# Moving the matmul operands by 64 bytes against each other in on-chip memory

## The chip, the cores and the metric

One core of a Trainium2 chip runs the whole program. The time is that of one execution on the device in microseconds (us), the median over runs. Five engines work side by side on a core: TensorE (in the profile PE, its weight loads PEld), VectorE (DVE), ScalarE (ACT), GpSimd (POOL) and SyncE (SP, which here only issues transfers).

## What is computed

Two network blocks in a row on a sequence of 256 tokens of width 2048, all in 32-bit floating point. Cut to the matrix products that fill the time:

```python
# first block
h = einsum('bsd,de->bse', x, w_in)            # 2048 -> 18688, in 16 pieces
merged = sum(sigmoid(g[i]) * (y[i] @ w_branch[i]) for i in range(4))   # 1024 -> 2048 each
x = layer_norm(ALPHA * x + merged @ w_out)
# second block
proj = rmsnorm(x) @ w_in_2                    # SSD and attention with forget gates
x = x + concat(y_ssd, y_fox) @ w_out_2
t = rmsnorm(x); q = t @ peer_wq               # picks 16 of 128 x 128 experts per head
x = x + (G * gelu(t @ u.T)) @ v               # all 16384 experts, G is zero where not picked
return rmsnorm(x)
```

## The kernel before

Every weight matrix is cut into chunks of 128 x 2048 numbers (1 MB). One list, `stream`, holds the 526 chunks in the order of the program, and one loop at the end of `_kern` (lines 1704 to 1720) goes through their halves. SyncE loads a chunk into `wr` (three buffers). For each half, ScalarE copies it into `wh`, rounded to the matmul's own 32-bit format, and VectorE puts the rest, `wr - wh`, into `wl` (`split`, line 292; four buffers each). The other operand is split into a high and a low part in the same way: `XH` and `XL` hold 16 x 256 numbers per partition (the normalized input, transposed), `YH` and `YL` 8 x 256 (the outputs of a branch). A product is then the sum of three matmuls: high by high, low by high, high by low.

There are four ways in which the halves are used. The text calls them T, Y, N and V:

- T (`T_chunk`, line 318): 128 columns of the weight half are loaded into the array and 256 columns of XH or XL stream past them. The trace names the streaming operand first: `XH,wh`, `XL,wh`, `XH,wl`.
- Y (`wb_chunk`, line 767): the same with YH and YL for `w_branch`, from the middle of the first block to its end.
- N (`N_chunk`, line 353): 128 columns of XH or XL are loaded and 512 columns of the weight half stream: `wh,XH` and so on. `w_out`, `w_out2` and some parts of the input projections are of this kind.
- V (`V_chunk`, line 1626): 128 columns of `whh` or `whl` (the weighted activations, split) are loaded and 512 columns of the weight half stream. It fills the last quarter of the program.

```python
for kk in range(8):                                                       # T_chunk
    k = half * 8 + kk
    PE.matmul(o, h[:, kk], XH[:, k], start=k == 0, stop=False)
    PE.matmul(o, h[:, kk], XL[:, k], start=False, stop=False)
    PE.matmul(o, l[:, kk], XH[:, k], start=False, stop=k == KT - 1)
```

TensorE takes its matmuls in program order. Between them stand smaller matmuls of the background work (attention, pooling, the choice of experts), which `bg()` puts in once in each half. Among these are `gb,ga` (in `g_gen`, line 1494), four at a time, 256 columns in the same format as the T matmuls, between two T matmuls of `uT`.

Tiles get their places in on-chip memory from pools, in the order in which the pools ask for them. The pool `per` (XH, XL, X, constants) comes first, then `wraw` with `wr`, `wspl` with `wh` and `wl`, and then the pools of the stages one over the other: `a1` with YH and YL, `a2`, `a3`, `w5`. Every tile that a matmul reads here is a multiple of 512 bytes long per partition, and the slices that one matmul takes begin at multiples of 512 bytes in it, so all matmuls of a kind see the same places modulo 512. In `a1` a tile `gap` of 704 bytes stands ahead of YH; the attention uses its first 64 bytes.

Of the kernel before, what the change touches and what calls it, by code (L numbers as in the profile page):

```python
# [6 lines left out]
F32 = mybir.dt.float32  # L7
# [9 lines left out]
P = 128  # L17
# [202 lines left out]
def kern(tc, A, out):  # L220
    nc = tc.nc
    with ExitStack() as ctx:
        ctx.enter_context(tc.manual_schedule())
        _kern(tc, nc, ctx, A, out)


def _kern(tc, nc, ctx, A, out):
    tasks = Tasks(4)
    V, SC, G, PE = Meter(nc.vector, tasks, "dve"), Meter(nc.scalar, tasks, "act"), nc.gpsimd, Meter(nc.tensor, tasks, "pe")
    per = ctx.enter_context(tc.tile_pool(name="per", bufs=1))  # L230
# [5 lines left out]

    XH = per.tile([P, KT, S], FR, name="XH")
    XL = per.tile([P, KT, S], FR, name="XL")
    X = [per.tile([P, D], F32, name=f"X{t}") for t in range(2)]
    cst = per.tile([P, 7, P], F32, name="cst")  # L240
    par = per.tile([P, N_PAR], F32, name="par")
# [13 lines left out]
    def pv(name, i=0, n=1):  # L255
        o, _ = PAR[name]
        return par[:, o + i:o + i + n]

    def row_ap(name):
        o, w = ROW[name]  # L260
        src = A["rows"]
        return bass.AP(tensor=src.tensor, offset=src.offset + o, ap=[[0, P], [1, w]])
# [55 lines left out]
    def T_chunk(evac):  # L318
        def fn(half, hi, lo):
# [5 lines left out]
            for kk in range(8):  # L325
# [4 lines that stand above are left out]
# [6 lines left out]
    def dtf_chunk(evac):  # L336
        def fn(half, hl, _):
# [4 lines left out]
            for kk in range(8):  # L342
                k = half * 8 + kk
                PE.matmul(o, w[:, kk], XH[:, k], start=k == 0, stop=False)
                PE.matmul(o, w[:, kk], XL[:, k], start=False, stop=k == KT - 1)
                if kk == 2:
# [6 lines left out]
    def N_chunk(kq, evac, korder=(0, 1, 2, 3), hold=False, lead=None):  # L353
        def fn(half, hi, lo):
# [6 lines left out]
            def part(t, kq, half, h, l):  # L361
                ts = slice(t * P, (t + 1) * P)
                for kk in range(2):
# [3 lines left out]
                    PE.matmul(ps[t], XH[:, k, ts], h[:, kk], start=first, stop=False)  # L367
                    PE.matmul(ps[t], XL[:, k, ts], h[:, kk], start=False, stop=False)
                    PE.matmul(ps[t], XH[:, k, ts], l[:, kk], start=False, stop=last)
# [45 lines left out]
    a1 = p1.enter_context(tc.tile_pool(name="a1", bufs=1))  # L415
    w1 = p1.enter_context(tc.tile_pool(name="w1", bufs=2))

    B4 = [a1.tile([P, 1024], F32, name=f"B4{i}") for i in range(4)]
    gap = a1.tile([P, 176], F32, name="gap")
    YH = a1.tile([P, 8, S], FR, name="YH")  # L420
    YL = a1.tile([P, 8, S], FR, name="YL")
    R = a1.tile([P, 8 * 286 + 8 * 272], F32, name="R")
# [7 lines left out]
    Q = VQ.rearrange("p (j t) -> p j t", j=8)  # L430
    U_ = X[0].rearrange("p (j t) -> p j t", j=8)
    GA = X[1].rearrange("p (j t) -> p j t", j=8)
    kT = a1.tile([P, S], F32, name="kT")
# [15 lines left out]
    def start_split():  # L449
        for g in range(4):  # L450
            SC.copy(XH[:, g * 4:(g + 1) * 4], xq[g])
            V.tensor_sub(XL[:, g * 4:(g + 1) * 4], xq[g], XH[:, g * 4:(g + 1) * 4].bitcast(F32))
            if g < 2:
# [87 lines left out]
    def conv_gen(ln):  # L541
# [13 lines left out]
        for stat in range(2):  # L555
# [4 lines left out]
            m = w1.tile([P, S], F32, name="cm")  # L560
            V.tensor_reduce(m, (sq if stat else CV).rearrange("p j t -> p t j"), axis=AX.X, op=OP.add)
            yield WAIT
# [102 lines left out]
    def attn_gen(u):  # L665
        def make(ln):
# [24 lines left out]
            m2 = sm[:, 0, :nq].rearrange("p (v j) -> p v j", v=2)  # L691
            V.tensor_reduce(sm[:, 0, :nq], L3, axis=AX.X, op=OP.max)
            V.tensor_tensor(m2, m2, sks, op=OP.max)
# [104 lines left out]
    for br, (_, need, ysrc) in enumerate(order):  # L798
# [4 lines left out]
        for jj in range(8):  # L803
            def pre_y(need=need, ysrc=ysrc, br=br):
# [5 lines left out]
                if br == 2:  # L810
                    nc.gpsimd.dma_start(X[0], A["xN"][0])
                    nc.gpsimd.dma_start(X[1], A["xN"][1])
                    nc.gpsimd.dma_start(GC.rearrange("p j t -> p (j t)"), row_ap("ln_g"))
# [16 lines left out]
    def split_M(a, b):  # L830
        for g in range(a, b, 2):
            s = slice(g, g + 2)
            SC.copy(XH[:, s], M[:, s])
            V.tensor_sub(XL[:, s], M[:, s], XH[:, s].bitcast(F32))

# [28 lines left out]
    def to_T(t, lnw, hooks={}):  # L864
        for k0 in range(0, KT, 2):
# [6 lines left out]
            for k in (k0, k0 + 1):  # L872
                V.scalar_tensor_tensor(XL[:, k, t * P:(t + 1) * P], p[:, k - k0], pv(lnw, k),
                                       hs[:, k - k0].bitcast(F32), op0=OP.mult, op1=OP.subtract)
# [964 lines left out]
```

## Time and profile before

| | |
|---|---|
| median of 3 runs | 3102.1 us (3099.98 to 3108.45) |
| the profiled execution, own time | 3096.91 us |
| its span, first to last instruction | 3095.2 us |
| mean granted clock of TensorE in it | 0.996 of 2.4 GHz |
| busy: TensorE, VectorE, ScalarE, GpSimd | 98%, 71%, 51%, 7% |
| read from main memory over the span | 601.53 MB |

The page of the profile gives busy time by engine, the chain of work that ended last (followed back from the last instruction), and the costliest groups of instructions with their count and mean duration. Matmuls are pipelined: a matmul of 256 columns is listed with some 280 ns, but the next one starts long before it ends. How fast they follow each other is read from a table by stretch, which counts the instructions of an engine in a stretch of time, or from the timeline.

### The profile page before, as it was taken

The numbers are of one execution on the slowest core, as the hardware profiler recorded it, in microseconds if no ns is written. First come the engines' busy times: TensorE is split into PE (matmuls) and PEld (weight loads), VectorE is DVE, ScalarE is ACT, GpSimd is POOL, SyncE is SP. The second block draws the span as 40 slices with busy tenths as digits, with TensorE's granted clock in tenths as the row PEclk, the third lists the DMA queues.
The fourth block names the chain that finished last, engine by engine and source line by source line (L and its number), as shares of the span: only waits on it lengthen the run. The fifth ranks groups of instructions, "written<-read, shape, count | busy, mean of one in ns | idle before, by whom it ended". The sixth has DMA issues, their size and how long they took to land.

```text
span 3095.2 us, 53096 instructions
## 1 busy us (share of the span) xinstructions
PE 3045.9 (98%) x21964; PEld 2843.4 (92%) x21964; DVE 2200.6 (71%) x3195; ACT 1575.5 (51%) x2199; POOL 220.2 (7%) x187
## 2 busy tenths in 40 slices
PE   8999999999999989998999999999999999999998
PEld 8899999999999869897899999999999888888887
DVE  8899865555555567766489989788796666666665
ACT  4443565434444445556454457667675444444444
POOL 0000000000000020100000012223140000000000
PEclk9999999999999989999999999999999999999999
DMA  7555555555555535434545665666658766666654
GB/s 274 184 196 198 180 190 188 196 189 203 182 202 191 184 129 180 175 130 143 190 150 189 220 218 197 253 250 220 254 203 326 275 243 229 247 246 250 241 215 150
DMA packets 92226, 640.61 MB, mean 207 GB/s; under 512 B 10272, under 2 KB 10448, under 8 KB 17744
## 3 DMA queue, kind: packets, MB, share of 16 engines
q1 hardware_dynamic: 78192, 559.06, 50.0%
q0 software_dynamic: 13504, 77.63, 6.9%
q8 instruction: 172, 2.82, 0.4%
q14 instruction: 70, 0.57, 0.1%
q10 hardware_dynamic: 288, 0.52, 0.0%
HBM read 601.53 MB, written 35.65 MB: 206 GB/s over the span
## 4 chain that ended last, share of the span: by engine, by line
PE 96%; DVE 2%; ACT 1%; issue 1%; DMA 0%; POOL 0%; SPq 0%; DVEq 0%; ACTq 0%
PE pm L216 92%; PE bg L216 4%; ACT wh L216 1%; DVE wl L216 0%; DMA wr<-w_in 0%; DVE X L216 0%; DVE XL L216 0%; POOL keys L1523 0%; DVE stg L216 0%; ACT XH L216 0%; DVE gb L216 0%; DVE PX L216 0%; ACT PX L216 0%; ACT L216 0%; ACT keys L216 0%
## 5 line engine op out<-in xcount | busy, mean ns | idle before, releaser
L216 DVE TENSOR_TENSOR wl<-wr,wh 128x1024 fp32r<-128x1024 f32 x1048 | 1291.0, 1234 | 820.5 <-ACT wh L216 817.0
L216 ACT CAST wh<-wr 128x1024 fp32r<-128x1024 f32 x1054 | 1109.0, 1053 | 1380.7 <-PE pm L216 1328.4
L216 PE MATMUL pm<-XH,wh 128*128 128x256 f32 x4976 | 1392.1, 280 | 8.3 <-ACT wh L216 8.3
L216 PE MATMUL pm<-XL,wh 128*128 128x256 f32 x4976 | 1382.1, 278 | 0.0
L216 PE MATMUL pm<-XH,wl 128*128 128x256 f32 x4960 | 1378.7, 278 | 0.9 <-DVE wl L216 0.9
L216 PEld LDWEIGHTS pm<-XH,wh 128*128 128x128 f32 x4976 | 940.8, 189 | 14.5 <-ACT wh L216 8.3
L216 PEld LDWEIGHTS pm<-XL,wh 128*128 128x128 f32 x4976 | 936.8, 188 | 1.0 <-issue 0.7
L216 PEld LDWEIGHTS pm<-XH,wl 128*128 128x128 f32 x4960 | 931.8, 188 | 1.4 <-DVE wl L216 1.4
L216 PE MATMUL pm<-wh,whl 128*128 128x512 f32 x1024 | 398.3, 389 | 0.0
L216 PE MATMUL pm<-wh,whh 128*128 128x512 f32 x1024 | 398.3, 389 | 0.0
L216 PE MATMUL pm<-wl,whh 128*128 128x512 f32 x1024 | 398.3, 389 | 0.0
L216 PEld LDWEIGHTS pm<-wl,whh 128*128 128x128 f32 x1024 | 192.2, 188 | 39.9
L216 PEld LDWEIGHTS pm<-wh,whl 128*128 128x128 f32 x1024 | 192.2, 188 | 39.9
L216 PEld LDWEIGHTS pm<-wh,whh 128*128 128x128 f32 x1024 | 192.2, 188 | 39.8
L216 PE MATMUL pm<-wh,XH 128*128 128x512 f32 x448 | 178.0, 397 | 0.0
L216 PE MATMUL pm<-wh,XL 128*128 128x512 f32 x448 | 176.7, 394 | 0.0
L216 PE MATMUL pm<-wl,XH 128*128 128x512 f32 x448 | 176.4, 394 | 0.0
L1523 POOL TENSOR_TENSOR keys<-cst,t 128x512 f32<-128x512 f32 x64 | 132.2, 2065 | 208.0 <-ACT ga L216 207.7
L216 PE MATMUL pm<-YH,wh 128*128 128x256 f32 x512 | 144.1, 281 | 0.0
L216 PE MATMUL pm<-YL,wh 128*128 128x256 f32 x512 | 143.7, 281 | 0.0
L216 PE MATMUL pm<-YH,wl 128*128 128x256 f32 x512 | 143.7, 281 | 0.0
L216 DVE SCALAR_TENSOR_TENSOR CV<-R,par,CV 128x256 f32<-128x256 f32 x240 | 117.0, 487 | 7.3
(288 smaller groups left out, 2371.3 us busy)
## 6 DMA issues: line engine op xcount, KB each, us to landing
wr<-w_in SPq DMA_DIRECT2D x190, 1024.0 KB, 4.8
wr<-uT SPq DMA_DIRECT2D x128, 1024.0 KB, 4.9
wr<-v SPq DMA_DIRECT2D x128, 1024.0 KB, 4.8
wr<-w_branch SPq DMA_DIRECT2D x32, 1024.0 KB, 4.8
wr<-w_out SPq DMA_DIRECT2D x32, 1024.0 KB, 4.8
wr<-wq SPq DMA_DIRECT2D x16, 1024.0 KB, 4.8
Ad<-ast POOLq DMA_DIRECT2D x16, 1024.0 KB, 5.1
Gd<-stg POOLq DMA_DIRECT2D x16, 1024.0 KB, 11.2
```

What stands on the lines that cost most here:

```text
L216: return f(out, *a, **k)
L1523: G.tensor_tensor(x, it, t3[:, 0, n0:n0 + 4, None].to_broadcast([P, 4, P]), op=OP.subtract)
```

## The change

The pool `per` gets an unused tile of 64 bytes behind XL, and `gap` loses 64 bytes, so that YH and YL and what lies behind them in `a1` keep their places.

```diff
     XH = per.tile([P, KT, S], FR, name="XH")
     XL = per.tile([P, KT, S], FR, name="XL")
+    per.tile([P, 16], F32, name="gapx")
     X = [per.tile([P, D], F32, name=f"X{t}") for t in range(2)]
...
     B4 = [a1.tile([P, 1024], F32, name=f"B4{i}") for i in range(4)]
-    gap = a1.tile([P, 176], F32, name="gap")
+    gap = a1.tile([P, 160], F32, name="gap")
     YH = a1.tile([P, 8, S], FR, name="YH")
```

Each engine's instructions, their order and what they wait for are the same before and after. What changes are places. In bytes modulo 512, from the start addresses in the two built programs:

| tile | before | after |
|---|---|---|
| XH, XL, YH, YL | 128 | 128 |
| wr, wh, wl | 448 | 0 |
| whh, whl (V) | 448 | 0 |
| ga, gb | 0 | 64 |
| streaming less loaded: T and Y | 192 | 128 |
| streaming less loaded: N | 320 | 384 |
| streaming less loaded: V, and gb,ga | 0 | 0 |

All other tiles of `per`, `a2`, `a3` and `w5` move by 64 bytes as well.

## Rows read from the trace of the kernel before

**Rows 1.** The profile's page: span, TensorE's busy time, and the chain's shares.

```profile
span 3095.2 us, 53096 instructions
...
PE 3045.9 (98%) x21964; PEld 2843.4 (92%) x21964; DVE 2200.6 (71%) x3195; ACT 1575.5 (51%) x2199; POOL 220.2 (7%) x187
...
PE 96%; DVE 2%; ACT 1%; issue 1%; DMA 0%; POOL 0%; SPq 0%; DVEq 0%; ACTq 0%
```

**Rows 2.** Costliest groups: out<-in, shape, xcount | busy us, mean ns | idle before.

```profile
L216 PE MATMUL pm<-XL,wh 128*128 128x256 f32 x4976 | 1382.1, 278 | 0.0
L216 PE MATMUL pm<-XH,wl 128*128 128x256 f32 x4960 | 1378.7, 278 | 0.9 <-DVE wl L216 0.9
...
L216 PE MATMUL pm<-wh,whl 128*128 128x512 f32 x1024 | 398.3, 389 | 0.0
...
L216 PE MATMUL pm<-wh,XL 128*128 128x512 f32 x448 | 176.7, 394 | 0.0
...
L216 PE MATMUL pm<-YL,wh 128*128 128x256 f32 x512 | 143.7, 281 | 0.0
```

**Rows 3.** Table by stretch, TensorE: stretch, length, busy (xcount), granted clock, DMA share, GB/s.

```profile
110.00:140.00 30.00, 30.00 (x132) 1.00 0.49 178
...
520.00:1030.00 510.00, 510.00 (x4333) 1.00 0.54 192
1050.00:1120.00 70.00, 70.00 (x302) 1.00 0.52 186
...
1700.00:1790.00 90.00, 90.00 (x796) 1.00 0.62 222
2500.00:2900.00 400.00, 400.00 (x1767) 1.00 0.66 244
```

**Rows 4.** Groups of two neighbouring stretches, 200.5 to 207.5 and 209 to 216 us.

```profile
L216 PE MATMUL pm<-XL,wh 128*128 128x256 f32 x21 | 5.8, 276 | 0.0
...
L216 PE MATMUL pm<-XL,wh 128*128 128x256 f32 x21 | 5.9, 281 | 0.0
```

**Rows 5.** Timeline, TensorE, around 510 us: start us, us, what (five and four rows left out).

```profile
509.81 0.28 PE L216 MATMUL pm<-XH,wl 128*128 128x256 f32 x1
...
510.49 0.28 PE L216 MATMUL pm<-XH,wl 128*128 128x256 f32 x1
510.69 0.66 PE L216 MATMUL bg<-B,vN 128*64 128x128 f32 x8
511.28 0.38 PE L216 MATMUL pm<-XH,wh 128*128 128x256 f32 x1
511.50 0.28 PE L216 MATMUL pm<-XL,wh 128*128 128x256 f32 x1
...
512.09 0.28 PE L216 MATMUL pm<-XH,wh 128*128 128x256 f32 x1
```

**Rows 6.** Timeline, TensorE, around the four gb,ga matmuls at 2042 us.

```profile
2041.83 0.28 PE L216 MATMUL pm<-XL,wh 128*128 128x256 f32 x1
2041.95 0.28 PE L216 MATMUL pm<-XH,wl 128*128 128x256 f32 x1
2042.06 0.64 PE L216 MATMUL bg<-gb,ga 128*128 128x256 f32 x4
2042.54 0.28 PE L216 MATMUL pm<-XH,wh 128*128 128x256 f32 x1
```

**Rows 7.** Timeline of the weight loads at the same place.

```profile
2041.95 0.54 PEld L216 LDWEIGHTS bg<-gb,ga 128*128 128x128 f32 x4
```

**Rows 8.** Splits (page), ScalarE's wait (waits: us, times, longest), a chunk's landing (last number).

```profile
L216 DVE TENSOR_TENSOR wl<-wr,wh 128x1024 fp32r<-128x1024 f32 x1048 | 1291.0, 1234 | 820.5 <-ACT wh L216 817.0
L216 ACT CAST wh<-wr 128x1024 fp32r<-128x1024 f32 x1054 | 1109.0, 1053 | 1380.7 <-PE pm L216 1328.4
...
ACT wh L216 <- PE pm L216: 1328.4, 914, 3.5
...
wr<-w_in SPq DMA_DIRECT2D x190, 1024.0 KB, 4.8
```

## The prediction

> **What bounds the kernel now.** I read the chain of work that ended last first [rows 1]: TensorE carries 96% of it and is busy for 98% of the span, so the kernel lasts as long as TensorE's sequence of matmuls lasts. Next the costliest groups [rows 2]: three kinds of matmul fill that sequence. "T" matmuls (XH or XL streams as the moving operand, 256 columns, a weight half is loaded) number 3 x 4976 less 16, that is 14912; the same with YH and YL 3 x 512 = 1536; "N" matmuls (the weight half streams, 512 columns, X is loaded) 1344; "V" matmuls (weight half against whh and whl, 512 columns) 3072. None of them has idle time to speak of in front of it. What remains is the time from one matmul's start to the next, its **step**.
>
> A step comes from the table by stretch [rows 3]: the stretch's length over its count, less about two matmuls that began before it. T matmuls take 90 us / 794 = 113.3 ns in one stretch and 510 us / 4331 = 117.8 ns in another, with the same tiles, the same shape and a granted clock of 1.00 in both. The row's duration goes with the step: 276 ns in the quick stretch, 281 in the slow one [rows 4]. Two neighbouring stretches of 7 us differ in the same way, so it isn't a matter of the stage of the program. The timeline shows where the step changes [rows 5]: before eight small matmuls of the attention the T matmuls start 0.11 or 0.12 us apart (0.68 us for six), after them 0.12 (0.59 us for five), and it then stays slow for over 500 us. So a stream of T matmuls settles into one of two rhythms and holds it until something breaks the stream. N matmuls also have two, 30 us / 130.5 = 229.9 ns and 70 us / 300.5 = 233 ns, V matmuls one, 400 us / 1765 = 226.6 ns [rows 3].
>
> What differs between these kinds, besides the width, is where their two operands lie. While a matmul streams its moving operand, the weights of the next one are read, as the row of the four loads of ga shows, which starts with the last T matmul [rows 6, 7]. By the table of places ahead, moving place less place of the loaded weights, modulo 512, is 192 for T, 320 for N, 0 for V and 0 inside the four gb,ga matmuls. Those four take 0.48 us together, 120 ns each [rows 6], at the T matmuls' width.
>
> **The change part by part.** No instruction is added, removed or moved; every operand from X0 to the weight halves lies 64 bytes further on.
> (1) T and Y matmuls go from 192 to 128. That is 16448 steps, all on the path. How many are slow now: XL,wh has 1382.1 us / 4976 = 277.8 ns and XH,wl 1378.7 / 4960 = 278.0, on average 277.9, so (277.9 - 276) / (281 - 276) = 0.37 of the T matmuls (with the means unrounded); YL,wh has 143.7 / 512 = 280.7, so 0.94 of the Y ones [rows 2, 4]. That makes 0.37 x 14912 + 0.94 x 1536 = 6960 slow steps, 42% of all, and 9490 quick ones, 117.8 - 113.3, some 4.4 ns, apart. Bounds for the step at 128: from below 113.3, as no row of this shape is quicker; from above 120, the four gb,ga matmuls [rows 6]. All at 113.3 saves 6960 x 4.4 = 31 us; all at 117.8 costs 9490 x 4.4 = 42 us; all at 120 costs 9490 x 6.7 + 6960 x 2.2 = 79 us. I take 113.3, because of the one place where the trace already has the relation 128: the last XH,wl before the gb,ga matmuls streams XH (place 128) while ga (place 0) is loaded. In the timeline it takes 0.11 us like its neighbours, and the slip comes only within the four that follow, which are at 0 [rows 6]. It is one matmul at a time, never a stream, so it shows that 128 needn't lose anything, not that a stream always holds the quick rhythm there.
> (2) N matmuls go from 320 to 384. From 226.6 (as V, at 0) to 233: of the 1344, the 384 of w_out lie in the slow stretch and 960 at 229.9, so all at 226.6 saves 384 x 6.4 + 960 x 3.3 = 6 us and all at 233 costs 960 x 3.1 = 3 us. I take 0, between the two, as no row is nearer.
> (3) V stays at 0 and the four gb,ga at 0: nothing.
> (4) VectorE and ScalarE write the weight halves to, and the transfers put wr at, the shifted places. The splits take 1234 and 1053 ns [rows 8] and most of ScalarE's wait is for TensorE to free a half (1328.4 us); a chunk of 1 MB lands in 4.8 us, while its 48 T matmuls take 5.44 us even at 113.3. So I cost these at nothing. If the splits' durations changed by 1%, it would show only where VectorE is near full, in the first 500 us and around 1600 to 1900 us: 1% of 1291 us is 13 us and under a third of it lies there, 4 us either way.
> What is late next: at 113.3 a chunk still takes longer than its transfer and than its two VectorE splits (2 x 1.23 us), so nothing takes the place of the lost 4.4 ns in the long streams. Sum: -31 us. The profiled execution took 3096.9 us beside a span of 3095.2, so 3066 for it; the median of the runs, 3102.1, stands 5 us above that, so **3071 us** for the changed kernel's median.
>
> **The rivals.**
> A. The slow rhythm becomes the rule: a stream at 128 settles into 117.8 ns after each break. It decides from the share of slow steps, 42% now; each further tenth costs 1645 x 4.4 = 7 us, so it is slower by over 0.3% (9 us, about what a measurement of this kernel can tell from no change) from 55% on, and at 100% the time is 3102 + 42 = 3144. For it: the long slow stretch shows that the slow rhythm is as steady as the quick one, and 128 is one step nearer to 0, where 256-column matmuls slip. Against it: the single matmul at 128.
> B. At 128 each T matmul collides fully with the weight load, as gb,ga at 0: 120 ns, 3102 + 79 = 3181. For it: gb,ga. Against it: the same single matmul, and V, which at 0 has the quickest step of its width.
> C. The relation has no bearing, and a stream's rhythm is drawn anew at each break by something else: the share of slow steps stays between 29 and 55%, 3102 within 9 us. For it: both rhythms exist at one and the same relation, 192, and the runs shown differ by 8.5 us among themselves. Against it: V never has two rhythms over 700 us, N never has V's step.
> The Trainium skill (TensorE: Matmul & The Clock Gate, "Step-by-step: what each phase is for") says that the streaming operand and the weight load have read ports of their own, so that loading the next weights takes nothing from the running matmul; by that rule the places of the operands don't matter and C is what remains. The trace speaks against it as far as a matmul of one shape has two steps at one clock, but it doesn't show which reader waits.
>
> **How the numbers follow.** The forecast (nearly all T matmuls quick; from 10 us of gain to 37 with N's best end) 0.50, A 0.25, B 0.13, C 0.12. Faster 0.50, same 0.12, slower 0.38. The range begins at 3071 - 6 (N's best end) - 3 (the spread of the runs below the median) = 3062. Upwards it takes in C and A with N's 3 us, 3147, and leaves out B alone. The forecast's own range is 3062 to 3092.
>
> **What would show it right or wrong.** If right, the table by stretch has about 885 T matmuls per 100 us in the long stream from 500 to 1000 us where 851 stand now, the groups XL,wh and YL,wh both have a mean near 276 ns, and the stretches after the attention's small matmuls no longer change step; V stays at 226.6. A is seen in means of 281 throughout, also in the stream from 1700 us on, which is quick now; B in a step of 120 and durations above 281. C shows as the same two steps with other borders. The forecast is wrong in its reason, if not in sign, if the T step falls below 113.3 (the floor would then not be a floor), or if the time moves without the counts per stretch moving, for example through VectorE's splits.

## The result, and the profile after

The changed kernel takes **3159.5 us** (median of 4 runs, 3158.1 to 3161.4) beside 3103.4 us (3100.0 to 3108.5) for the kernel before: a ratio of 1.0182, with an interval of 1.0170 to 1.0194. It is 56 us slower where 31 us of gain were forecast, and lies 12 us above the range, between the rivals A (3144) and B (3181).

The page of the profile after: TensorE bounds the kernel as before and has taken up all of the difference. Its busy time rose by 68.5 us, the span by 63 [rows 1]; the splits on VectorE and ScalarE, 1236 and 1051 ns, stand where they stood [rows 8]; ScalarE waits 48 us more for TensorE.

```profile
span 3158.1 us, 53096 instructions
...
PE 3114.4 (99%) x21964; PEld 2909.9 (92%) x21964; DVE 2209.2 (70%) x3195; ACT 1576.2 (50%) x2199; POOL 195.4 (6%) x187
...
L216 DVE TENSOR_TENSOR wl<-wr,wh 128x1024 fp32r<-128x1024 f32 x1048 | 1292.7, 1236 | 873.3 <-ACT wh L216 868.3
L216 ACT CAST wh<-wr 128x1024 fp32r<-128x1024 f32 x1054 | 1107.2, 1051 | 1440.2 <-PE pm L216 1376.7
...
L216 PE MATMUL pm<-XL,wh 128*128 128x256 f32 x4976 | 1403.3, 282 | 0.0
...
L216 PE MATMUL pm<-wh,whl 128*128 128x512 f32 x1024 | 398.3, 389 | 0.0
...
L216 PE MATMUL pm<-wh,XL 128*128 128x512 f32 x448 | 177.4, 396 | 0.0
...
L216 PE MATMUL pm<-YL,wh 128*128 128x256 f32 x512 | 144.1, 281 | 0.0
```

Against [rows 2] only two kinds moved: the T matmuls from 278 to 282 ns, and N by 2 ns. V is the same to a tenth of a microsecond. The table by stretch of the same kernel (stretch, length, busy and count, granted clock, DMA share, GB/s) turns that into steps:

```profile
110.00:140.00 30.00, 30.00 (x131) 1.00 0.54 193
520.00:1030.00 510.00, 510.00 (x4304) 1.00 0.54 190
1065.00:1135.00 70.00, 70.00 (x303) 1.00 0.52 183
1700.00:1790.00 90.00, 90.00 (x752) 1.00 0.57 203
2600.00:3000.00 400.00, 400.00 (x1766) 1.00 0.66 243
```

Taking off two of each count (one and a half for N) for the matmuls that began before the stretch, as for [rows 3], a T step is 510 us / 4302 = 118.6 ns where it was 117.8, and 90 us / 750 = 120.0 ns in a part of `uT`, where it was 113.3. N, which had 229.9 and 233, now has 30 us / 129.5 = 232 and 70 us / 301.5 = 232. V has 400 us / 1764 = 226.8 ns. The granted clock is 1.00 in every one of these stretches, before and after, so the difference isn't the clock's.

The chain of waits shows the same without counting edges (start us, length us, what): first the kernel after, then the kernel before.

```profile
224.20 8.55 PE pm L216 x72
...
527.13 620.94 PE pm L216 x4863
...
1589.23 250.03 PE pm L216 x2089
```

```profile
190.64 8.48 PE pm L216 x72
...
511.35 617.34 PE pm L216 x4863
...
1561.84 238.54 PE pm L216 x2089
```

A piece of 72 T matmuls, 8.55 / 72 = 118.8 ns each, is barely longer than a slow one before (8.48). The long piece from 511 us on was slow before too and lost 4 us; the one in `uT` was quick and lost 11.5 us.

Summed over the trace, from the start of each matmul to the start of the next (us; the next may be one of another kind, or come after a wait):

| kind | steps | before | after |
|---|---|---|---|
| T and Y | 16448 | 1914.8 | 1974.5 |
| N | 1344 | 335.7 | 338.8 |
| V | 3072 | 696.1 | 696.1 |
| the rest | 1100 | 131.4 | 131.8 |

So 60 of the 63 us are T's and Y's, 3 are N's. 36 of the 60 lie in the 6912 steps of `wq` and `uT`, most of which were quick before.

### The profile page after: what moved, and what is told of

It reads as the page before. It is cut to its first block, busy times and chain, and to the rows that moved or that the text cites. A ratio compares the mean times of both kernels' runs of the same rounds, so it can differ in the third digit from the quotient of the medians.

```text
span 3158.1 us, 53096 instructions
## 1 busy us (share of the span) xinstructions
PE 3114.4 (99%) x21964; PEld 2909.9 (92%) x21964; DVE 2209.2 (70%) x3195; ACT 1576.2 (50%) x2199; POOL 195.4 (6%) x187
## 4 chain that ended last, share of the span: by engine, by line
PE 97%; DVE 1%; ACT 1%; issue 1%; DMA 0%; SPq 0%; DVEq 0%; ACTq 0%
PE pm L216 93%; PE bg L216 4%; DMA wr<-w_in 0%; ACT wh L216 0%; DVE wl L216 0%; DVE X L216 0%; DVE XL L216 0%; ACT XH L216 0%; DVE PX L216 0%; ACT PX L216 0%; ACT L216 0%; SPq L442 0%; DVE keys L216 0%; ACT RB L216 0%; ACT t L216 0%
## 5 line engine op out<-in xcount | busy, mean ns | idle before, releaser
L216 DVE TENSOR_TENSOR wl<-wr,wh 128x1024 fp32r<-128x1024 f32 x1048 | 1292.7, 1236 | 873.3 <-ACT wh L216 868.3
L216 ACT CAST wh<-wr 128x1024 fp32r<-128x1024 f32 x1054 | 1107.2, 1051 | 1440.2 <-PE pm L216 1376.7
L216 PE MATMUL pm<-XH,wh 128*128 128x256 f32 x4976 | 1414.7, 284 | 8.0 <-ACT wh L216 8.0
L216 PE MATMUL pm<-XL,wh 128*128 128x256 f32 x4976 | 1403.3, 282 | 0.0
L216 PE MATMUL pm<-XH,wl 128*128 128x256 f32 x4960 | 1401.0, 282 | 0.7 <-DVE wl L216 0.7
L1524 POOL TENSOR_TENSOR keys<-cst,t 128x512 f32<-128x512 f32 x64 | 109.0, 1703 | 243.0 <-ACT ga L216 242.8
```

What stands on the lines that cost most here:

```text
L216: return f(out, *a, **k)
L1524: G.tensor_tensor(x, it, t3[:, 0, n0:n0 + 4, None].to_broadcast([P, 4, P]), op=OP.subtract)
```

## The experiments

**The theory:** a stream's step depends on the relation, the place of the streaming operand less that of the loaded one, and 128 is a worse one than 192. **The rivals:** other tiles that moved by 64 bytes (the halves, X, the tiles of the stages) cost the time; the relation only matters beside the other engines' traffic; the slow rhythm belongs to certain stages of the program.

### Streams by themselves

The edit is a kernel of its own: 48 matmuls at a time of T's format and width, five such streams for each relation, with one to five small matmuls (`brk`) ahead of each. The loaded operand lies at place 0 ("a") or 64 ("b").

```python
for sub in range(5):
    brk(sub + 1)
    for i in range(n):
        PE.matmul(p[:m, :width], st[:, s0 + (i % 8) * P:s0 + (i % 8) * P + m],
                  mv[:, d + k * width:d + (k + 1) * width], start=i == 0, stop=i == n - 1)
```

> No part of the reference is computed: the kernel is 27 kinds of matmul stream alone, each kind five times 48 (or 30) matmuls after one to five small 32-bit matmuls, with the other engines idle. Theory (the relation, streaming place less loaded place modulo 512, decides which rhythms a stream can take): 256 columns: relation 192 gives 113.3 or 117.8 ns from stream to stream, 128 gives 118.5 to 120, 0 gives 120; 512 columns: 0 gives 226.7, 320 gives 229.9 or 233, 384 gives 232 to 233; the same at both places of the loaded operand (a and b). With half as many columns loaded (H) the loss shrinks. Rival 1 (the splits and transfers that run beside the matmuls make the loss): every 256-column stream has 113.3 here and every 512-column one 226.7, whatever the relation. Rival 2 (the place of the loaded operand alone decides): a and b differ at one and the same relation.

The timeline, TensorE (start us, length us, what); the number behind the T is the relation.

```profile
28.56 6.00 PE L53 MATMUL T0a<-mv,st 128*128 128x256 f32 x48
...
85.92 5.94 PE L53 MATMUL T128a<-mv,st 128*128 128x256 f32 x48
...
111.42 5.90 PE L53 MATMUL T192a<-mv,st 128*128 128x256 f32 x48
...
124.29 5.70 PE L53 MATMUL T192a<-mv,st 128*128 128x256 f32 x48
...
149.47 6.00 PE L53 MATMUL T256a<-mv,st 128*128 128x256 f32 x48
...
251.86 5.70 PE L53 MATMUL T448a<-mv,st 128*128 128x256 f32 x48
...
341.23 5.94 PE L53 MATMUL T128b<-mv,st 128*128 128x256 f32 x48
```

From the starts of the settled matmuls in them, lengths of 5.70, 5.90, 5.94 and 6.00 us are steps of 113.3, 117.8, 118.7 and 120.0 ns. By relation (the very first stream of the program, whose first steps took 213 ns, is left out):

| relation | steps of the five streams, ns |
|---|---|
| 0, 256 | 120.0 |
| 64, 320 | 117.8, seldom 113.3 |
| 128, 384 | 118.7, all five |
| 192, 448 | 113.3 and 117.8, two or three of each |

The streams "b" give the same steps, so it is the relation and not the place. With the other engines idle, that leaves the traffic of VectorE, ScalarE and the transfers out of it. The quick rhythm that the forecast puts at 128 doesn't occur there at all, and 192, where the kernel before stands, is the one at which a stream takes either rhythm. 512 columns behave alike (0: 226.7, 64: 229.0, 128: 232.3 to 233.5, 192: 233.3 ns) and also repeat after 256 bytes: N went from 320, which is 64, to 384, which is 128.

One part missed. With half as many columns loaded (64), relation 0 gives 113.3 in all five streams, 128 gives 116.6 and 120.0, and 192 some 119.0. Half a load doesn't make the loss smaller: it makes another relation the good one.

### The relation alone, and the rest of the move alone

In the first kernel XH, XL, YH and YL move back by 64 bytes, and every other tile keeps its place modulo 512: the change's relation of T and Y (and N's), with nothing else of its move.

```diff
+    per.tile([P, 112], F32, name="gapw")
     XH = per.tile([P, KT, S], FR, name="XH")
     XL = per.tile([P, KT, S], FR, name="XL")
+    per.tile([P, 16], F32, name="gapx")
...
-    gap = a1.tile([P, 176], F32, name="gap")
+    gap = a1.tile([P, 160], F32, name="gap")
...
+    a1.tile([P, 16], F32, name="gapy")
```

> XH, XL, YH and YL go to place 64, the weight halves and all else stay at their places modulo 512: relation 128 as in the changed kernel, 384 for N. Theory (relation): 3160 us, within 10 us of the changed kernel, T steps of 118.5 to 120 ns. Rival 2 (the place of the weight halves, or of the other tiles that moved, decides): 3103 us as before.

In the second, all tiles move by 64 bytes together: the halves, X and the stages' tiles stand at the change's places modulo 512 (but for those from YH on in `a1`, which the change leaves in place), and the relation stays 192.

```diff
+    per.tile([P, 16], F32, name="gapw")
     XH = per.tile([P, KT, S], FR, name="XH")
```

> All tiles go 64 bytes on, XH, XL, YH and YL too: weight halves at 0 as in the changed kernel, relation 192 and 320 as before. Theory (relation): 3103 us within 10, T steps of 113.3 and 117.8 ns. Rival 2 (the places of the halves and the other tiles): 3160 us.

The first takes 3160.6 us, ratio 1.0178 (1.0161 to 1.0195); the second 3099.4 us, ratio 0.999 (0.998 to 1.000). The table by stretch, the first kernel and then the second:

```profile
520.00:1030.00 510.00, 510.00 (x4308) 1.00 0.54 190
1700.00:1790.00 90.00, 90.00 (x761) 1.00 0.59 205
```

```profile
520.00:1030.00 510.00, 510.00 (x4332) 1.00 0.54 192
1700.00:1790.00 90.00, 90.00 (x797) 1.00 0.62 217
```

The relation alone brings the whole loss, the rest of the move nothing. That settles rival C as well: the relation has a bearing. The Trainium skill (TensorE: Matmul & The Clock Gate, "Step-by-step: what each phase is for"), by whose port rule C was what remained, doesn't agree with these rows, nor with the bare streams (113.3 to 120.0 ns by relation, at one shape and with the other engines idle).

### Two more relations in the whole kernel

An unused tile as in the change, but of 256 bytes, makes the relation of T and Y 448.

```diff
     XL = per.tile([P, KT, S], FR, name="XL")
+    per.tile([P, 64], F32, name="gapx")
...
-    gap = a1.tile([P, 176], F32, name="gap")
+    gap = a1.tile([P, 112], F32, name="gap")
```

> Weight halves at 192, X and Y at 128: relation 448, which is 192 plus 256. Theory, as the single streams repeat after 256 bytes: T in the two steps of 113.3 and 117.8 ns, N (64) as before; 3103 us within 10, or up to 3144 if the draw of the rhythms after the breaks changes. Rival (the whole 512 counts): no forecast from the relation 192.

With larger ones it becomes 256, that is 0 if the steps repeat after 256 bytes.

```diff
     XL = per.tile([P, KT, S], FR, name="XL")
+    per.tile([P, 112], F32, name="gapx")
...
-    gap = a1.tile([P, 176], F32, name="gap")
+    gap = a1.tile([P, 64], F32, name="gap")
```

> Weight halves at 384, X and Y at 128: relation 256, as 0. Theory: all T and Y steps at 120.0, 16286 x (120 - 115.2) = 79 us more than before, N at 226.7, 5 us less: 3177 us. Rival (the loss needs the exact distance 0 or 128 to 192): not slower than the changed kernel's 3160.

Relation 448 takes 3102.8 us, ratio 0.9993 (0.9981 to 1.0004); 256 takes 3168.8 us, ratio 1.0209 (1.0192 to 1.0226). The table by stretch, 448 and then 256:

```profile
520.00:1030.00 510.00, 510.00 (x4332) 1.00 0.55 192
1700.00:1790.00 90.00, 90.00 (x767) 1.00 0.60 211
```

```profile
520.00:1030.00 510.00, 510.00 (x4260) 1.00 0.53 188
1070.00:1140.00 70.00, 70.00 (x310) 1.00 0.55 196
1700.00:1790.00 90.00, 90.00 (x753) 1.00 0.54 193
```

So the period of 256 bytes holds in the kernel: 448 acts as 192, and 256 as 0, with 510 us / 4258 = 119.8 ns for T and 70 us / 308 = 227 ns for N, its best. The forecast for 256 was 8 us too high. In the stretch from 1700 us on, relation 448 has a step of 90 us / 765 = 117.6 where relation 192 has 113.3, with the time over all the same: which rhythm a stream holds is not fixed by the stage.

### What makes a stream change its rhythm

To the kernel before, one to three small matmuls are added ahead of 14 chunks of `w_branch` (their result isn't used).

```diff
-        return f if br == 0 and jj >= 4 else None
+        return f if br == 0 and jj >= 4 else (lambda: poke(1 + jj % 3)) if br >= 2 else None
+    def poke(n):
+        p = pm.tile([P, 512], F32, name="pm")
+        for _ in range(n):
+            PE.matmul(p[:, :P], ident, tri, start=True, stop=True)
```

> The kernel before with one to three small 32-bit matmuls (128 columns, output unused) put in ahead of 14 of the w_branch chunks in the later half of the long slow stream, some 3 us of added matmuls in all. Theory (a stream holds its rhythm until it is broken and draws it anew at the break): up to the first of them the stream stays at 117.8 ns as before, behind them some of the 14 pieces have 113.3 and some 117.8, each from its break to the next. Rival (that stage of the program is slow by itself, from the work beside it): all pieces stay at 117.8.

One run took 3101.7 us, beside 3105.4 us for the kernel before, which tells nothing of a difference; the steps are what it was run for. The table by stretch, from the long slow stretch on; the rows begin and end between the places, and the fourth row shown holds one of them, at 853 us:

```profile
520.00:730.00 210.00, 210.00 (x1786) 1.00 0.55 191
736.00:766.00 30.00, 30.00 (x267) 1.00 0.54 180
769.00:784.00 15.00, 15.00 (x130) 1.00 0.50 155
...
838.00:910.00 72.00, 72.00 (x638) 1.00 0.55 193
915.00:946.00 31.00, 31.00 (x266) 1.00 0.54 178
```

The steps are 117.7, 113.2, 117.2, 113.2 and 117.4 ns. The timeline at the first place shows the turn (one added matmul stands there as two records): steps of 0.12 us up to 734.20, and, not shown, 0.11 and 0.12 in turn from 734.55 on.

```profile
734.08 0.28 PE L216 MATMUL pm<-XH,wl 128*128 128x256 f32 x1
734.20 0.39 PE L216 MATMUL pm<-cst 128*128 128x128 f32 x2
734.35 0.37 PE L216 MATMUL pm<-YH,wh 128*128 128x256 f32 x1
734.55 0.28 PE L216 MATMUL pm<-YL,wh 128*128 128x256 f32 x1
```

A stretch that was slow from end to end is now quick in between, with the same tiles at the same places: the rival that the stage is slow by itself falls. At 192 each break decides the rhythm anew, which is held to the next one. It looks like a rule rather than chance: from the starts, the pieces behind one, two and three small matmuls have 113.3, 113.3 and 117.8 ns, the same once more, then 113.3 and 113.3; after a longer piece that ends at 913 us it is 117.8, 117.8 and 113.3, twice.

### A place that the breaks can't disturb

Since the three matmuls of a T group need not have one relation, streams of T's groups of three were run at 64 combinations, eight streams each: XH at a, XL at b, `wh` at 0, `wl` at c.

```python
PE.matmul(o, h, xh, start=k == 0, stop=False)
PE.matmul(o, h, xl, start=False, stop=False)
PE.matmul(o, l, xh, start=False, stop=k == 11)
```

> No part of the reference is computed: streams of T groups of three (h by XH, h by XL, l by XH) with XH at place a, XL at b, h at 0 and l at c, each of a, b, c one of 0, 64, 128, 192, eight streams of 36 matmuls each after one to eight small 32-bit matmuls, other engines idle. Theory: with a = b and c = 0 the steps are those of the single streams (0: 120; 64 and 192: 113.3 or 117.8 from stream to stream; 128: 118.7). If the collision of a matmul with the next load is decided matmul by matmul, a mixed group has the mean of its three relations, a, b - c, a, and none beats 113.3 for all eight streams. If instead the rhythm is a lock between neighbours, some mixed groups fall into 113.3 in every stream, since a matmul at another place takes the stream out of the slow lock.

The answer for one tile (least, median and longest duration in ns, first and last start; the name is a x b x c, the rows are those of the second matmul of the group):

```profile
L61 PE MATMUL R192x192x128t<-m,st x96: 276/276/284, 2641.5 to 2681.8; 128*128 128x256 f32 x96
```

```profile
L61 PE MATMUL R192x192x0t<-m,st x96: 276/281/282, 2557.4 to 2598.2; 128*128 128x256 f32 x96
```

By the starts, 192x192x128 alone was quick, 113.3 ns, in all eight streams. 192x192x0, the kernel before, was quick in four of eight and 117.8 in the others; 128x128x0, the changed kernel, 118.6 to 118.8 in all. 64x64x128 was quick in seven. A mixed group isn't decided by the relation of each streaming operand to the weights loaded next: 192x64x128 has 192 in all three places by that count, and took 121.1 ns in every stream, more than any single relation.

A third kernel of bare streams went through relations in steps of 16 bytes for 256 columns, and through places of N's operands for 512.

> No part of the reference is computed: streams with the other engines idle. First N groups of three (512 columns, h, h and l streaming past X loaded) with X at place a and l at place c, h at 0, in steps of 64; then single 256-column streams at relations 0 to 240 in steps of 16. Theory (a collision between neighbours, periodic in 256 bytes): a = 0, c = 0 gives 226.7, a = 192, c = 0 gives 229, and moving l by 128 changes N and V groups too, so that the change that holds T in its quick step must leave them alone; the single streams that start off the multiples of 32 have no step below 113.3. Rival: some start between gives fewer than 113.3, then the floor is not one.

No stream of 256 columns went below 113.3 ns. Relation 192 again gave 113.3 or 117.8, and the others, but for 112, lay between 116.6 and 120.1. Relation 112 began each of its six streams with some ten steps of about 118 ns and then held 113.3 to the end. One stream's early and late matmuls in the timeline (one of 0.28 us ends each row, so the steps are 0.95 us / 8 = 118.8 ns and 2.49 us / 22 = 113.2 ns):

```profile
846.70 1.23 PE L71 MATMUL T112t<-mv,st 128*128 128x256 f32 x9
```

```profile
847.99 2.77 PE L71 MATMUL T112t<-mv,st 128*128 128x256 f32 x23
```

So a single relation can hold the quick rhythm after every break that was tried as well; in the whole kernel 112 was not run.

For N with X at 192 the step is 229 in five streams of six as long as `wl` has the place of `wh`, and 230 to 231 with `wl` at 128, so N's chunks should keep `wl` where it is.

So in the kernel before, `wl` gets 256 bytes more, and T and Y chunks put it 128 bytes further in; N and V chunks (`fn.place`, set in `N_chunk` and `V_chunk`) don't.

```diff
-        l = wspl.tile([P, HALF], FR, name="wl")
+        o = getattr(stream[c][2], "place", 32)
+        l = wspl.tile([P, HALF + 64], FR, name="wl")[:, o:o + HALF]
...
+        fn.place = 0
```

> All places as in the kernel before, except that wl is kept 128 bytes further on in its buffer where a T or Y chunk uses it (each wl buffer grows by 256 bytes); N and V chunks keep theirs. Theory (lock between neighbours, taken from the mixed streams with XH, XL at 192 and l at 128): every T and Y step at 113.3, 30 us off: 3073 us within 8, clearly faster than before. Rival 1 (a mixed group is a mean of its relations, 192, 64, 192): 3100 to 3110. Rival 2 (the idle surroundings of the streams mattered): the two rhythms stay and so does the time, 3103.

It takes **3070.8 us** (6 runs, 3068.3 to 3073.4) beside 3102.9 us, ratio 0.9902 (0.9885 to 0.9918), and is the quickest of all: 89 us below the changed kernel. Its table by stretch, its groups and its chain:

```profile
510.00:1005.00 495.00, 495.00 (x4371) 1.00 0.57 200
1700.00:1790.00 90.00, 90.00 (x796) 1.00 0.62 220
2500.00:2900.00 400.00, 400.00 (x1767) 1.00 0.66 242
```

```profile
L216 PE MATMUL pm<-XL,wh 128*128 128x256 f32 x4976 | 1377.0, 277 | 0.0
...
L216 PE MATMUL pm<-YL,wh 128*128 128x256 f32 x512 | 141.6, 277 | 0.0
```

```profile
190.81 8.18 PE pm L216 x72
...
507.64 595.74 PE pm L216 x4863
```

The long stream has 495 us / 4369 = 113.3 ns, the 72 matmuls of one piece 8.18 us where they took 8.48 and 8.55. V is unchanged. Summed as above, T and Y take 1888.4 us, 26 less than before, and N 334.6. Two of this kernel's relations are 192, and the third, `XH,wl`, is 64 (taken against the weights loaded next, it is `XL,wh` that has 64); by themselves both showed the slow rhythm as well. That the mixture holds the quick one after every break was found by trying, and no run here explains it.

## Why the prediction was wrong

**What bounds the kernel** was right: TensorE's steps, and nothing else moved.

**Step (1), T and Y, failed**, at the words "I take 113.3, because of the one place where the trace already has the relation 128". A bare stream at 128 takes 118.7 ns. Put into that step's own sum, this gives 9490 x (118.7 - 113.3) + 6960 x (118.7 - 117.8) = 57 us, and 3102 + 57 = 3159, the time measured. That it fits to a microsecond is luck in part: the sum leaves out the pieces at 120.0 ns and N's 3 us, and the profiled executions differ by 63 us where the medians differ by 56. The count of slow steps was good (42%; by the starts it is 40% in the unbroken pieces), and the steps measured at 128 lie within the bounds. What was chosen between the bounds was not sound, for two reasons:

- The single matmul was misread. The prediction went by starts in hundredths of a microsecond, in which a step of 113.3 ns and one of 118.7 differ by half a digit. In whole nanoseconds, the matmul at 128 takes 117 ns to the next start, where the six before it take 113 or 114; at 58 of the 64 such places in the trace it takes 117 or 118. So the one place at 128 spoke, if anything, against 113.3. The row of that stretch (one `XH,wl` ahead of gb,ga, of the kernel before) has 278 ns for the matmul in question and 276 for those before it:

```profile
L216 PE MATMUL pm<-XH,wl 128*128 128x256 f32 x1 | 0.3, 278 | 0.0
L216 PE MATMUL pm<-XH,wh 128*128 128x256 f32 x1 | 0.3, 276 | 0.0
```

- Whatever its step, it stood between a quick stream and four matmuls at 0. The prediction called it "never a stream" and gave it the weight all the same. At 192 one place and one shape already have two rhythms, so a single step can't tell which of them a stream takes up.

The upper bound of 120 was read as coarsely: the four gb,ga matmuls take 473 ns, 118 each. That 120.0 is the step at 0 was shown only by the bare streams.

**The gain itself was there**: 31 us for "all at 113.3", against 26 us in the profiled executions (3096.9 and 3070.4) once `wl` was moved, which is what T and Y lost. The medians differ by 32, as the profiled execution of the kernel before was one of its quickest; that the median of this other kernel is the 3071 of the forecast is partly luck. The size was about right, and 128 was the wrong place to look for it.

**Steps (2) to (4).** N cost 3 us, as much as the upper bound named for it, where 0 was taken: relation 384 acts as 128, and there the bare streams have 232.3 to 233.5 ns, near the slower of N's two steps before. V and the splits cost nothing, as forecast. The 3 us that the range takes for the spread of the runs below the median are 2.1 in the three runs named (3102.1 less 3099.98), which decides nothing.

**The rivals.** A (117.8 everywhere, +42 us) and B (120 everywhere, +79) both named what happens, that no stream at 128 is quick; together they had 0.38. In the whole kernel a stream at 128 has two rhythms of its own, 118.7 and 120.0 ns, and holds one from break to break, so A's step is a little too short and B's is that of a part of the program. From 1700 us the changed kernel has 120.0 where the kernel with the same relation and the halves left in place has 90 us / 759 = 118.6; at the end of `uT` it is the other way round, 60 us / 506 = 118.6 and 60 us / 500 = 120.0 (first the changed kernel, then the other):

```profile
2391.00:2451.00 60.00, 60.00 (x508) 1.00 0.89 342
```

```profile
2392.00:2452.00 60.00, 60.00 (x502) 1.00 0.90 345
```

No bare stream at 128 had 120.0, and why the kernel has it is open. The argument for A, that 128 is nearer to 0, where 256 columns slip, was better than the argument against it, though the steps don't fall evenly with the distance: 64 and 192 differ, and 112, once settled, holds 113.3 beside 118.7 at 128. "Against" B stood V, quickest of its width at 0: that was no evidence, since 256 and 512 columns have their good and bad relations apart (0 is the best for 512 and the worst for 256).

**C** had it that both rhythms at one relation mean that the relation has no bearing. Both things are true at once: at 192 the breaks decide the rhythm, and the relation sets which rhythms there are.

## What to carry to other kernels

Where TensorE's steps bound a kernel and one stream shows two steps at one clock, shape and stage, compare the places of the streaming and the loaded operand modulo 256 bytes: between the best and the worst single relation lay 6% of a step for 256 columns, and 3% of the time between the quickest and the slowest kernel here. Which place is good depends on the widths and on how matmuls alternate, so sweep it with bare streams of the kernel's own pattern, each begun after breaks of different length and long enough to settle, and take a place that is quick after all of them. A single matmul between two others doesn't show what a stream of its kind settles into, and starts printed in hundredths don't show a difference of a few nanoseconds.

## What the runs showed that was not expected

- The steps repeat after 256 bytes, not after 512: the kernel took 3102.8 us at 448 beside 3103.4 at 192, and the streams at 256 and 384 have the steps of 0 and 128.
- At 2.4 GHz the quickest steps, 113.33 and 226.67 ns, are 272 and 544 cycles, 17/16 of the columns; no stream went below. 120.0 ns is 288 cycles, and three steps of 117.8 are 848: all of these are multiples of 16 cycles.
- At relation 192 a stream of T matmuls has two steady rhythms, and a small matmul in it is enough to change from one to the other (117.7 to 113.2 ns after a single one) for as long as nothing breaks it again. With bare streams the same break gives the same rhythm: in all three kernels of bare streams, with the loaded operand at 0, the streams behind one to five small matmuls are quick, slow, slow, quick, quick. How a break decides it, no run here shows.
- Loading 64 columns instead of 128 makes 0 the quickest relation (113.3 ns) and 192 a slow one (119.0). So the weight load has a part in it. Which of the two reads waits, no run here shows.
- N at its own best relation, 0, beside T at its best was not tried; with 227 ns a step against 230 the estimate from these steps is some 1344 x 3 ns = 4 us. Nor was relation 112 for T and Y, which held 113.3 ns in all six bare streams after some ten slow steps each.
